# Attention traced without raised scheduling priority in a one-core attention and mLSTM layer

## The chip, the core and the metric

The kernel runs on one core of a Trainium2 chip. The metric is the device time of one execution in microseconds (us). A core has five engines with a queue each: TensorE (PE, the matmuls; its weight loads are shown as PEld), VectorE (DVE), ScalarE (ACT), GpSimd (POOL) and SyncE (SP, which issues most DMAs). Each engine runs its own instructions in the order in which they stand in its queue; between engines semaphores make an instruction wait.

## The reference

One layer of a diffusion backbone: 128 prompt tokens and 1024 latent tokens, width 1024. From one normalised input it projects grouped-query attention (8 query heads of 64, 2 key/value heads) and a bidirectional mLSTM (4 heads of 128, in chunks of 128 tokens), joins both by an output projection, and ends with a SwiGLU FFN of width 2816.

```python
def attention(q, k, v):              # blocks of 128 queries
    def one_block(qi):
        s = jnp.einsum('bqhgd,bkhd->bhgqk', qi, k).astype(F32) * ATTN_SCALE
        p = jax.nn.softmax(s, axis=-1).astype(v.dtype)
        return jnp.einsum('bhgqk,bkhd->bqhgd', p, v)
...
def trunk_layer(...):
    h = rmsnorm(x, norm1_w) * (1 + sc1) + sh1
    aq, ak, av, mq, mk, mv, mo, mg = jnp.split(h @ w_in, SPLIT_POINTS, axis=-1)
    ...
    attn_o = attention(aq, keys, vals)
    ...
    hm, st_f, st_b = mlstm_bidir(heads(mq), heads(mk) * (MLSTM_DK ** -0.5), heads(mv), gates, init_f, init_b)
    ...
    x = x + g1 * (jnp.concatenate([attn_o, hm], axis=-1) @ w_out)
    h2 = rmsnorm(x, norm2_w) * (1 + sc2) + sh2
    x = x + g2 * swiglu(h2, w_gu, w_down)
```

The prompt's queries see the 128 prompt keys; the latent queries see 1024 latent keys and 128 cached ones, 1152 in all.

## The kernel before

**Who sets the order.** The kernel is written as Python generators, each of which emits some instructions and yields. `weave` and `beside` step a main generator and take steps of side generators between its own, at given rates. What is emitted is a trace; a scheduler then simulates the engines and picks for each engine, among the instructions that are ready in its simulation, the one with the best place in the traced order. `hot(n)` (line 59) is `tc.high_priority(n)`: what is traced inside it gets a place n instructions ahead of where it was traced. So the final order of every queue hangs on these numbers. Instructions outside such a block keep their traced place.

**Attention** (`attention`, line 1088) is a side generator. The nine blocks of 128 queries are cut in three chunks of three, `attention(0..2)`, and `chain` puts them one behind the other. The first block is the prompt's. For each of the eight heads of a block:

- six matmuls write the scores S of 128 x 1152 into PSUM (line 1129); there is one buffer for S, so the next head's scores must wait until the exp has read the last one;
- DVE takes the row maximum (1131), ACT the exponential with its row sum into `pr` (1132), DVE two tiny operations for the scale (1133, 1134);
- ACT writes the weights' float16 high part `ph` (1135), DVE the remainder `pl` (1136);
- SP issues a transposing DMA for each, to `phT` (1138) and `plT` (1139).

For each pair of heads a group of 18 matmuls then multiplies the transposed weights with the values (1153 with phT, 1154 with plT, in turn), and ACT and DVE copy the result out (1156, 1158). The generator emits a pair's values one step after the scores of the next pair's second head, so that the transposes have time. In the text the 72 head passes are called S1 to S72 and the 36 values groups V1 to V36, in the order of the program; Vn belongs to S2n-1 and S2n. At the start of a block the queries are transposed by PE (124).

The first parameter after `done`, `ha`, is the priority of the queries, scores, softmax and transposes; the second, `hv`, that of the values group. Before, chunks 0 and 1 have 200 and 0, and chunk 2 has the defaults 200 and 200.

**What runs beside it.** The main work in the order of the program:

- the mLSTM heads: `head_project` (projection products, lines 526 to 528, and 866 to 868) and `head_mlstm` (products 842, 912 to 915, 946, 953), with one attention step for every four or five steps of them;
- the output projection of the first chunk, woven with the last mLSTM scan;
- the prefill of the first FFN chunk, with an attention step at every third of its steps;
- the first FFN pass: gate and up products (1473 to 1475), down products (1215 to 1217), with the splitting of each weight tile into a high part `whi` (ACT, line 174) and a low part `wlo` (DVE, line 145). `attention_side` is woven into it: first the output projection of chunk 1, then what is left of attention.

When attention has ended, its pools are closed, and the second FFN pass begins.

Of the kernel before, what the change touches and what calls it, by code (L numbers as in the profile page):

```python
# [33 lines left out]
CB = 3  # L34
# [15 lines left out]
def hybrid_step(ctx: ExitStack, tc: tile.TileContext, I: dict, O: dict):  # L50
# [15 lines left out]
    def weave(main, side, n_main, n_side):  # L66

        due = 0.0
        for units in main:
            due += n_side / n_main * (units or 1)  # L70
            while due >= 1.0:
                next(side, None)
                due -= 1.0
# [5 lines left out]
    def chain(*gens):  # L79
        for g in gens:  # L80
            for v in g:
                yield v
# [34 lines left out]
    o_d = [drp.tile([P, 512], F32, name=f"o_d{i}") for i in range(2 * CB)]  # L117
# [872 lines left out]
    def beside(*sides):  # L990

        due = [0.0] * len(sides)
        while True:
            for i, (g, rate) in enumerate(sides):
                due[i] += rate
                while due[i] >= 1.0:
                    next(g, None)
                    due[i] -= 1.0
            yield
# [737 lines left out]
    oT = []  # L1737
    done = set()
    o1 = []
    att0 = attention(0, oT, done, 200, 0)  # L1740
    o2 = []
    att = chain(att0, attention(1, o1, set(), 200, 0, o_d[0:CB]), attention(2, o2, set(), spill=o_d[CB:]))
    weave(head_project(0, sts[0]), beside((chain([None] * 10, att), 0.2),), 96, 96)
    for h in range(1, NH):
        scan = head_mlstm(h - 1, sts[h - 1])
# [176 lines left out]
```

## Time and profile before

| | |
|---|---|
| runs, us | 1533.99, 1530.81, 1533.54 |
| median, us | 1533.54 |
| profiled execution, us | 1534.27 |
| its span, us | 1532.5 |
| PE busy | 1429.3 us, 93% of the span, 8282 matmuls |
| DVE, ACT, POOL busy | 74%, 53%, 14% |

A row of the timeline reads: start (us from the span's start), duration, engine, line, operation, what it writes <- what it reads, shapes, how many in a row, and in brackets how long the engine stood idle before it and what released it. SPq is the issue of a DMA on SP's queue. A row of the stretches lists start and end, then for each engine the busy us and the number of its instructions, then PE's granted clock (1.00 is full speed), the share of the DMA engines' time, and GB/s. Starts of matmuls lie closer than their durations, since PE overlaps them.

### The profile page before, as it was taken

What the parts mean: (1) busy time and instruction counts of PE and PEld (TensorE: products, weight loads), DVE (VectorE), ACT (ScalarE), POOL (GpSimd) and SP (SyncE); (2) the same over time, 40 slices, a digit from 0 to 9 for tenths busy, and PEclk for the clock granted to TensorE, in tenths of its full rate; (3) what the DMA queues carried; (4) which work ended last, traced back from release to release, by engine and by line L of the source; (5) the groups of instructions that cost most, each with busy time, mean ns of one, the idle gap of its engine ahead of it and who ended that gap; (6) DMA issues with size and microseconds to landing.
All of it is one profiled execution on the core that took longest, in us unless ns stands there. A gap on an engine that the chain in (4) does not pass through costs nothing. (4 is left out here: it accounts for less than half of the span.)

```text
span 1532.5 us, 22792 instructions
## 1 busy us (share of the span) xinstructions
PE 1429.3 (93%) x8282; PEld 1064.6 (69%) x8282; DVE 1129.3 (74%) x2280; ACT 812.6 (53%) x1525; POOL 213.8 (14%) x310
## 2 busy tenths in 40 slices
PE   6889999998899789999999889999999999999994
PEld 3635667766677567978998777976766667676763
DVE  4968556775767978658677755979878696886857
ACT  4854467956767646555575743844334151523233
POOL 0122423231224345210100000000000000000000
PEclk9999999999999999999999989999999999999998
DMA  9575224653477774758687733444222140412112
GB/s 370 157 217 183 80 70 75 128 110 56 95 152 163 190 213 106 205 177 213 174 195 174 174 92 131 131 142 155 69 80 87 31 134 1 138 49 76 35 35 83
DMA packets 254182, 197.02 MB, mean 129 GB/s; under 512 B 166830, under 2 KB 208006, under 8 KB 254070
## 3 DMA queue, kind: packets, MB, share of 16 engines
q1 hardware_dynamic: 251070, 189.56, 45.7%
q10 hardware_dynamic: 2872, 5.62, 1.1%
q8 instruction: 65, 1.06, 0.3%
q14 instruction: 47, 0.39, 0.1%
q0 software_dynamic: 128, 0.39, 0.1%
HBM read 143.94 MB, written 13.26 MB: 103 GB/s over the span
## 5 line engine op out<-in xcount | busy, mean ns | idle before, releaser
L1621 PE MATMUL mm<-Bt,A 128*128 128x384 f16 x616 | 200.8, 326 | 0.0
L1620 PE MATMUL mm<-Bt,A 128*128 128x384 f16 x616 | 199.5, 326 | 0.8 <-DVE c L1641 0.8
L1622 PE MATMUL mm<-Bt,A 128*128 128x384 f16 x616 | 197.6, 326 | 0.0
L174 ACT CAST whi<-raw 128x1024 fp32r<-128x1024 f32 (+1 forms) x102 | 102.8, 1012 | 138.9 <-DMA raw<-in_w_down_dram 50.7
L145 DVE TENSOR_TENSOR wlo<-raw,whi 128x1024 fp32r<-128x1024 f32 (+1 forms) x102 | 121.4, 1190 | 52.2 <-ACT whi L174 46.5
L1136 DVE SCALAR_TENSOR_TENSOR pl<-pr,st,ph 128x1152 f16<-128x1152 f32 (+1 forms) x72 | 95.7, 1329 | 36.2 <-ACT ph L1135 36.2
L1473 PE MATMUL mm<-aTh,whi 128*128 128x384 f32 x352 | 120.6, 343 | 1.5 <-DVE F L1564 1.1
L1475 PE MATMUL mm<-aTh,wlo 128*128 128x384 f32 x352 | 120.0, 341 | 0.0
L1474 PE MATMUL mm<-aTl,whi 128*128 128x384 f32 x352 | 119.7, 340 | 0.0
L1132 ACT ACTIVATE pr<-S,st 128x1152 f32<-128x1152 f32 (+1 forms) x72 | 81.5, 1132 | 53.9 <-DVE st L1131 52.7
L1131 DVE TENSOR_REDUCE st<-S 128x1 f32<-128x1152 f32 (+1 forms) x72 | 88.8, 1234 | 22.7 <-PE S L1129 22.6
L526 PE MATMUL wi<-headw,hT 128*128 128x384 f16 x288 | 94.6, 328 | 1.2 <-ACT th L816 1.2
L1129 PE MATMUL S<-kst,qT 128*128 128x384 f32 (+1 forms) x400 | 87.6, 353 | 7.8 <-ACT pr L1132 7.8
L527 PE MATMUL wi<-headw,hT 128*128 128x384 f16 x288 | 94.6, 328 | 0.0
L528 PE MATMUL wi<-headw,hT 128*128 128x384 f16 x288 | 94.5, 328 | 0.0
L1135 ACT ACTIVATE ph<-pr,st 128x1152 f16<-128x1152 f32 (+1 forms) x72 | 83.8, 1163 | 17.1 <-DVE st L1134 8.4
L1620 PEld LDWEIGHTS <-A 128*128 128x128 f16 x616 | 60.2, 98 | 42.6 <-issue 3.3
L1621 PEld LDWEIGHTS <-A 128*128 128x128 f16 x616 | 60.3, 98 | 39.9 <-issue 0.9
L1622 PEld LDWEIGHTS <-A 128*128 128x128 f16 x616 | 60.2, 98 | 39.9
L1606 ACT ACTIVATE A<-S,six 128x1024 f16<-128x1024 f32 x44 | 49.9, 1145 | 68.6 <-PE mm L1622 54.8
L1204 DVE TENSOR_TENSOR t<-mm,hmr 128x512 f32<-128x512 f32 x84 | 54.3, 683 | 39.7 <-PE mm L1690 33.3
L1129 PEld LDWEIGHTS S<-kst,qT 128*128 128x128 f32 x400 | 70.4, 192 | 11.7 <-ACT pr L1132 9.5
(460 smaller groups left out, 3691.7 us busy)
## 6 DMA issues: line engine op xcount, KB each, us to landing
raw<-in_w_gu_dram SPq DMA_DIRECT2D x88, 512.0 KB, 3.6
raw<-in_w_down_dram SPq DMA_DIRECT2D x40, 512.0 KB, 3.9
a<-in_w_ada_dram SPq DMA_DIRECT2D x24, 512.0 KB, 5.5
iraw<-in_w_in_dram SPq DMA_DIRECT2D x32, 256.0 KB, 3.4
x<-in_x_sample_dram SPq DMA_DIRECT2D x11, 512.0 KB, 5.9
raw<-in_w_out_dram SPq DMA_DIRECT2D x10, 512.0 KB
aw<-in_w_ada_dram SPq DMA_DIRECT2D x8, 512.0 KB, 5.4
aw<-in_w_ada_dram SPq DMA_DIRECT2D x16, 256.0 KB, 7.9
```

The source lines that it names most:

```text
L145: (dve if eng == "dve" else pool).tensor_tensor(out=out, in0=full, in1=hi, op=ALU.subtract)
L174: nc.scalar.copy(hi[:, :n], raw[:, :n])
L526: mm(ps[:, :n], ah, wh[:, k % 2, c0 : c0 + n], start=(k == 0), stop=False)
L527: mm(ps[:, :n], ah, wl[:, k % 2, c0 : c0 + n], start=False, stop=False)
L1129: mm(S[:, n, 0:w], qT[:, h, :], kst[kv][:, t, c0 + n * w : c0 + (n + 1) * w], start=(t == 0), stop=(t == 1))
L1136: dve.scalar_tensor_tensor(out=plv, in0=prv, scalar=st[:, 3:4], in1=phv, op0=ALU.mult, op1=ALU.subtract)
L1473: mm(ps, wh[:, k, :], th[:, k, :], start=(k == 0), stop=False)
L1474: mm(ps, wh[:, k, :], tl[:, k, :], start=False, stop=False)
L1475: mm(ps, wl[:, k, :], th[:, k, :], start=False, stop=(k == KD - 1))
L1620: mm(ps, wh[:, k], bt[:, 0, k], start=first and k == 0, stop=False, skip_group_check=True)
L1621: mm(ps, wh[:, k], bt[:, 1, k], start=False, stop=False, skip_group_check=True)
L1622: mm(ps, wl[:, k], bt[:, 0, k], start=False, stop=k == 3, skip_group_check=True)
```

## The change

Attention of all three chunks gets `ha` = 0 and `hv` = 0: no instruction of it is traced inside a raised priority. Nothing else is edited.

```diff
-    att0 = attention(0, oT, done, 200, 0)
+    att0 = attention(0, oT, done, 0, 0)
     o2 = []
-    att = chain(att0, attention(1, o1, set(), 200, 0, o_d[0:CB]), attention(2, o2, set(), spill=o_d[CB:]))
+    att = chain(att0, attention(1, o1, set(), 0, 0, o_d[0:CB]), attention(2, o2, set(), 0, 0, o_d[CB:]))
```

So of chunks 0 and 1 the queries, scores, softmax and transposes lose their 200 places, and of chunk 2 the values groups too. The same instructions are issued; the order of rows changes on all five queues from the first attention block to the end of the first FFN pass. Three places follow. A row is the line, the operation, and written <- read; `S` are scores, `kst` keys, `qT` queries, `wi` the result of a projection, `mm` or `po` other results in PSUM; numbers tell tiles apart.

PE in the second mLSTM head's stretch, from S15 (S_584) to S16 (S_604), before:

```order
L1129 MATMUL S_584_3406<-kst1_1040,qT_442_2821 128x384 x6
L527 LDWEIGHTS hT2_452
L527 MATMUL wi_641_3648<-headw2_1845,hT2_452 128x384
...
L528 MATMUL wi_641_3648<-headw3_1846,hT2_452 128x384
L842 MATMUL mm_592_3438<-wv_591_3435,kt_585_3421 128x258
L946 MATMUL mm_596_3448<-cs_343_2417,qT_251_1991 128x129
L946 MATMUL mm_596_3448<-cs_381_2559,qT_251_1991 128x129
L1129 MATMUL S_604_3480<-kst1_1040,qT_442_2821 128x384 x6
```

And now:

```order
L1129 MATMUL S_584_3406<-kst1_1040,qT_442_2821 128x384 x6
L527 LDWEIGHTS hT2_452
L527 MATMUL wi_641_3648<-headw3_1846,hT2_452 128x384
L528 LDWEIGHTS hT2_452
L528 MATMUL wi_641_3648<-headw3_1846,hT2_452 128x384
L842 MATMUL mm_592_3438<-wv_591_3435,kt_585_3421 128x258
L946 MATMUL mm_596_3448<-cs_343_2417,qT_251_1991 128x129
L946 MATMUL mm_596_3448<-cs_381_2559,qT_251_1991 128x129
L1129 MATMUL S_604_3480<-kst1_1040,qT_442_2821 128x384 x6
```

Eight projection products stood between the two scores, and two stand there now: S15 has moved back past six of them, S16 has not moved.

PE at the end of attention, from S71 (S_1966) to V35 (po_1972), before:

```order
L1473 MATMUL mm_2010_10101<-aTh_1453_7241,whi_2013_10104 128x384
L1474 MATMUL mm_2010_10101<-aTl_1454_7242,whi_2013_10104 128x384
L1475 MATMUL mm_2010_10101<-aTh_1453_7241,wlo_2014_10105 128x384
L1129 MATMUL S_1966_9811<-kst1_1040,qT_1881_9437 128x384 x6
L1129 MATMUL S_1971_9830<-kst1_1040,qT_1881_9437 128x384 x6
L1153 LDWEIGHTS vs_1038
L1153 MATMUL po_1972_9845<-phT_1944_9736,vs_1038 128x256
```

And now, a little earlier, around S70 (S_1957), with V34 (po_1958):

```order
L1129 MATMUL S_1950_9742<-kst1_1040,qT_1881_9437 128x384 x6
L1474 MATMUL mm_1994_10004<-aTl_1454_7242,whi_2000_10040 128x384
...
L124 MATMUL mm_2007_10085<-ident_91,t2_2006_10083 128x128 x4
L1153 LDWEIGHTS vs_1038
L1153 MATMUL po_1958_9782<-phT_1915_9608,vs_1038 128x256
L1129 MATMUL S_1957_9767<-kst1_1040,qT_1881_9437 128x384 x6
L1154 LDWEIGHTS vs_1038
L1154 MATMUL po_1958_9782<-plT_1916_9609,vs_1038 128x256
```

Before, the end was S69, 17 gate/up products, V34 (18 products), S70, four transposes, 24 gate/up products, S71, S72, V35, V36. Now it is S69, five gate/up products, the four transposes, the first product of V34, S70, the other 17 of V34, 17 gate/up products, S71, seven gate/up products, V35, S72, V36.

DVE at the same place, as one piece of the difference (- before, + now):

```order
+L1158 SCALAR_TENSOR_TENSOR oS_1941_9700<-po_1972_9845,vsc_100,ol_1973_9864 64x128 x2
+L1131 TENSOR_REDUCE st_1970_9829<-S_1971_9830 128x1
 L1136 SCALAR_TENSOR_TENSOR pl_1964_9809<-pr_1962_9807,st_1965_9810,ph_1963_9808 128x1152
-L1131 TENSOR_REDUCE st_1970_9829<-S_1971_9830 128x1
 L1133 RECIPROCAL st_1970_9829<-st_1970_9829 128x1
 L1134 TENSOR_SCALAR st_1970_9829<-st_1970_9829 128x1
-L1158 SCALAR_TENSOR_TENSOR oS_1941_9700<-po_1972_9845,vsc_100,ol_1973_9864 64x128 x2
 L1136 SCALAR_TENSOR_TENSOR pl_1969_9828<-pr_1967_9826,st_1970_9829,ph_1968_9827 128x1152
```

The maximum of S72 has moved ahead of `pl` of S71, and V35's copy out ahead of both.

## The prediction

> **What bounds the kernel now.** I read the profile page first, then stretches of 25 us for the engines, then what TensorE (PE) waited for, then single instructions on PE, VectorE (DVE), ScalarE (ACT) and the SP queue. The page's busy line and two lines of its slices:
>
> ```profile
> PE 1429.3 (93%) x8282; PEld 1064.6 (69%) x8282; DVE 1129.3 (74%) x2280; ACT 812.6 (53%) x1525; POOL 213.8 (14%) x310
> PE   6889999998899789999999889999999999999994
> PEclk9999999999999999999999989999999999999998
> ```
>
> PE is busy for 93% of the span, so a new order of the same 8282 matmuls can only change where PE stands still. The change can act only from the first attention block to the end of the first FFN pass, about 900 us. The stretches (start:end, length, busy time of PE, weight loads, DVE, ACT, POOL, then granted clock, DMA share, GB/s):
>
> ```profile
> 275.00:300.00 25.00, 22.67 (x148) 16.62 (x146) 19.28 (x37) 23.16 (x61) 6.73 (x16) 1.00 0.75 169
> 425.00:450.00 25.00, 25.00 (x171) 18.51 (x169) 16.70 (x39) 15.70 (x40) 7.29 (x18) 1.00 0.53 103
> 825.00:850.00 25.00, 25.00 (x150) 22.62 (x149) 20.72 (x30) 16.59 (x25) 0.00 (x0) 1.00 0.82 206
> 850.00:875.00 25.00, 19.69 (x115) 18.14 (x114) 17.31 (x26) 20.82 (x30) 2.60 (x2) 0.96 0.77 177
> 875.00:900.00 25.00, 15.22 (x68) 11.58 (x67) 11.91 (x26) 9.84 (x18) 0.00 (x0) 0.70 0.32 71
> ```
>
> Where PE is full (425 to 450 us, and in the FFN pass 825 to 850), attention lies wholly beside other matmuls and a better order has nothing to win. What can be won is at the places where PE ran out of other work: spots in the mLSTM heads such as 275 to 300 us, and 850 to 900 us, the tail of attention, where the last FFN products of the pass have been used up. What PE waited for from 300 to 920 us (total us, times, longest):
>
> ```profile
> PE S L1129 <- ACT pr L1132: 7.0, 5, 3.8
> PE po L1153 <- DMA phT<-ph: 5.6, 2, 5.3
> PE mm L1153 <- DMA phT<-ph: 3.5, 2, 2.2
> PE mm L1153 <- ACT th L816: 2.4, 1, 2.4
> PE po L1154 <- DMA plT<-pl: 2.6, 3, 1.1
> PE mm L1154 <- DMA plT<-pl: 1.2, 2, 1.0
> ```
>
> Attention's own waits are these two kinds: a score group that waits for the exp of the head before it (there is one score buffer), and a values group that waits for the transposed weights. They sum to 22.3 us: more than that the change cannot give, and most of it stands in the tail.
>
> **How long the two chains are.** Number the 72 head passes S1 to S72 and the 36 values groups V1 to V36 (V of pair n belongs to S2n-1 and S2n). One score to the next, at S15 and S16:
>
> ```profile
> 275.14 1.35 PE L1129 MATMUL S<-kst,qT 128*128 128x384 f32 x6
> 276.94 1.36 DVE L1131 TENSOR_REDUCE st<-S 128x1 f32<-128x1152 f32 x1
> 278.69 1.24 ACT L1132 ACTIVATE pr<-S,st 128x1152 f32<-128x1152 f32 x1
> 276.33 0.34 PE L527 MATMUL wi<-headw,hT 128*128 128x384 f16 x1
> 276.50 0.33 PE L528 MATMUL wi<-headw,hT 128*128 128x384 f16 x1
> 280.08 1.32 PE L1129 MATMUL S<-kst,qT 128*128 128x384 f32 x6 [0.76 <-ACT pr L1132]
> ```
>
> S15 ends at 276.49, the max and the exp follow, and S16 starts at 280.08: 3.6 us between two scores are the price of the chain here, with 0.76 of it not covered. The best it could be is the max and the exp alone, 1.36 + 1.24 = 2.6; with DVE busy elsewhere it is longer (6.4 at S67, below). Score to values, at S34:
>
> ```profile
> 434.62 1.35 PE L1129 MATMUL S<-kst,qT 128*128 128x384 f32 x6
> 436.79 1.35 DVE L1131 TENSOR_REDUCE st<-S 128x1 f32<-128x1152 f32 x1
> 438.18 1.22 ACT L1132 ACTIVATE pr<-S,st 128x1152 f32<-128x1152 f32 x1 [0.35 <-DVE st L1131]
> 440.43 1.26 ACT L1135 ACTIVATE ph<-pr,st 128x1152 f16<-128x1152 f32 x1
> 441.73 1.42 DVE L1136 SCALAR_TENSOR_TENSOR pl<-pr,st,ph 128x1152 f16<-128x1152 f32 x1 [0.68 <-ACT ph L1135]
> 443.17 1.31 SPq L1139 DMA_TRANSPOSE plT<-pl  x1
> phT<-ph SPq DMA_TRANSPOSE x26, 3.4
> plT<-pl SPq DMA_TRANSPOSE x25, 3.7
> ```
>
> From 435.97 to 443.17 + 3.7 = 446.9 are 10.9 us. Back to back with no queue the pieces are 1.35 + 1.22 + 1.26 + 1.42 + 3.7 = 9.0.
>
> **The change part by part.** No instruction is added or removed; rows change places on all five queues. I count the PE work that the order puts between the end of one score group and the next, or its values, before and after, with the spacings of the trace: 0.17 us for a projection (276.33 to 276.50), 25.00/150 = 0.17 for a gate/up product, 0.11 for a values product (345.12 to 345.23, below). Where the work is shorter than the chain, PE waits for the rest.
>
> *Removed.* Three waits of the heads:
>
> ```profile
> 345.12 0.27 PE L1154 MATMUL mm<-plT,vs 128*128 128x256 f16 x1 [0.99 <-DMA plT<-pl]
> 345.23 0.27 PE L1153 MATMUL mm<-phT,vs 128*128 128x256 f16 x1
> 359.37 0.28 PE L1153 MATMUL mm<-phT,vs 128*128 128x256 f16 x1 [2.21 <-DMA phT<-ph]
> 400.43 1.32 PE L1129 MATMUL S<-kst,qT 128*128 128x384 f32 x6 [1.60 <-ACT pr L1132]
> ```
>
> S30 (400.43) has 2.1 us of work ahead of it before and 6.2 after: its 1.60 goes. V11 (345.12) gets 9.2 us for 8.7, and V12 (359.37) 6.3 for 5.8: 0.5 each. Sum -2.6. Nothing is late behind S30, because S31 now follows it more closely, which I count next.
>
> *New score waits in the heads,* at 3.6 us per chain. S16 loses six projections of its cover, 6 x 0.17 = 1.0, and it waited already, so all of that is paid: +1.0. S13 goes from 6.0 to 3.1 us of cover: +0.5. S31 from 5.4 to 3.0: +0.6. S39 from 3.8 to 2.4: +1.2. Sum +3.3. If the chain took its bare 2.6 us, S16 would pay about 1.0 and S39 0.2; at S67's length each of the four would pay about 3. What is queued behind each is more PE work of the heads, a product of the mLSTM (L953) first, and so the mLSTM waits with it.
>
> *New values waits in the heads,* at 10.9. V17 goes from 10.9 to 9.7 (+1.2), V18 from 12.1 to 10.4 (+0.5), V19 from 11.9 to 9.4, of which S39's own wait pays 1.2 (+0.3), V6 from 13.7 to 10.8 (+0.1). Sum +2.1. At 9.0 us all four are nothing; at V27 to V32 of the FFN pass, where the distances move by tens of us, nothing comes near a limit.
>
> *First FFN pass up to 850 us.* PE is full, so there is no wait to remove. DVE and ACT are not free, though; at S67:
>
> ```profile
> 834.78 1.22 PE L1129 MATMUL S<-kst,qT 128*128 128x384 f32 x6
> 839.11 1.35 DVE L1131 TENSOR_REDUCE st<-S 128x1 f32<-128x1152 f32 x1
> 841.18 1.20 ACT L1132 ACTIVATE pr<-S,st 128x1152 f32<-128x1152 f32 x1
> ```
>
> From 836.00 to 842.38 the chain takes 6.4 us, because the splits of the weights (L174, L145) stand ahead of it. The order puts 5.1 us before S68 where there were 8.5: +1.3. V33 has 13.6 us for 15.8 in a stage where the score's chain is some 3 us over its bare length, so 10.9 + 3.2 = 14.1: +0.5. Sum +1.8; bounds 0 (a chain of 3.6) and +4.
>
> *The tail.* Its rows before:
>
> ```profile
> 854.41 1.22 PE L1129 MATMUL S<-kst,qT 128*128 128x384 f32 x6
> 872.59 1.96 PE L1129 MATMUL S<-kst,qT 128*128 128x384 f32 x6 [3.79 <-ACT pr L1132]
> 885.08 0.37 PE L1153 MATMUL po<-phT,vs 128*128 128x256 f16 x1 [5.34 <-DMA phT<-ph]
> 886.33 0.39 PE L1154 MATMUL po<-plT,vs 128*128 128x256 f16 x1 [0.88 <-DMA plT<-pl]
> ```
>
> From the end of S69 (855.6) V36 starts 29.5 us later. In the new order I follow the chain from there. Five gate/up products, four transposes and one product of V34 take 1.6 us; S70 waits until 3.6 and ends at 4.8. The rest of V34 (17 x 0.11) and 17 gate/up products end at 9.6; S71 ends at 10.8, seven products at 12.0. V35 needs the weights of S70: 4.8 + 10.9 = 15.7, and ends at 17.7 (18 x 0.11). Only then comes S72, ending at 18.9. Its chain to the landing of ph's transpose took 885.08 - 874.55 = 10.5 us before, where S72's max stood behind pl of S71 on DVE and its ph behind V35's copy on ACT. In the new order the max is ahead of pl of S71, and V35's copy is ahead of everything. The bare chain is 1.35 + 1.22 + 1.26 + 3.4 = 7.2, and with the 1.42 of pl of S71, which still stands ahead of the reciprocal, 8.6; between that and 10.5 I take 9.4. V36 then starts at 28.3, that is 1.2 earlier than 29.5. Two waits are moved, from S72 (3.79) and V36 (5.34) to S70 (2.0), V35 (3.7) and V36 (9.4); the matmuls are the same. If S70's chain is as slow as S67's, 2.8 us over, the tail is 1.6 longer than before; with both chains bare it is 4 shorter. I take -1.
>
> Sum: -2.6 + 3.3 + 2.1 + 1.8 - 1.0 = **+3.6 us**. The profiled execution took 1534.27 us (span 1532.5 and 1.77 around it), so 1537.9; the median of the runs, 1533.54, lies 0.73 below that execution, which gives **1537.1**.
>
> **The clock.** After V12's wait of 2.21 us the next 3.4 us ran at:
>
> ```profile
> 360.40:363.80 3.40, 3.21 (x18) 2.27 (x17) 0.42 (x1) 0.87 (x4) 0.00 (x0) 0.59 0.01 2
> ```
>
> So a wait of 2.2 us costs 0.41 x 3.4 = 1.4 us more here. The Trainium skill, in TensorE: Matmul & The Clock Gate, section "HAM oscillation — how this bites in real kernels", puts the limit at idle gaps of about 3.4 us; by that rule the new waits of the heads would leave the clock alone and the sum would stay. The trace's 0.59 after 2.21 us does not bear this rule out.
>
> **The rivals.** *The chains are shorter than I took them, and the tail is won* (faster). With the scores at 2.6 us and the values at 9.0, the new waits shrink to S16 and S39, +1.2, those of the FFN pass to 0, and the tail gives its 4: -2.6 + 1.2 - 4 = -5.4, 1528. It decides from a score chain below 3 us and a values chain below 9.5. For it: ACT and DVE do the work of the mLSTM earlier, so its waits could shrink too (the wait on th L816, 2.4, is one I left alone). Against: 10.9 and 3.6 were measured in these same stages. Chance 0.25.
>
> *The waits take each other's place.* A wait paid at S13 or S39 gives the following chains the same time, as I reckoned only at V19; removed and new waits of the heads then cancel (-2.6 + 3.3) and so do FFN pass and tail: 1534, within 0.2%. That is also the outcome if the new order is as good as the old and nothing else. For it: the full stretches, and the same total of work. Chance 0.30.
>
> *The new waits take the clock down* (slower still). S16 then waits 0.76 + 1.0 = 1.8 us and its neighbour before it 0.4, S39 and V19 1.5 within 10 us: two places near the 2.21 us of V12, 1.4 us each, and in the tail S70 and V35 wait before the FFN products that ran at 1.0 before S72: 17 + 7 of them at 0.59, 24 x 0.17 x 0.7 = 2.8. Sum 3.6 + 2.8 + 2.8 = +9.2, 1543. It decides from waits of about 2 us. Against: the 0.76 of S16 left 1.00 in its stretch, 275 to 300 us, and a shorter chain undoes it. Chance 0.15.
>
> **How the numbers follow.** The forecast has 0.30: 1537, its own range 1534.5 to 1541. A measurement of this kernel can tell about 0.2%, 3.1 us: 1530.5 to 1536.6 counts as the same. The forecast lies on that border, with a third of its chance in the same band. Faster: 0.25 from the first rival, less a fifth that stays within the band, plus a little from the second: 0.24. Slower: 0.2 + 0.15 + 0.05 from the second: 0.40. Same: 0.36. The range from 1528 to 1544 takes in the price at bare chains and that with the clock.
>
> **What would show it.** S30 without its wait; S16 with about 1.8 us and S39 with 1.2 on the exp; V17 and V18 with about a us on their transposes; S68 with a wait in a stretch that was full; in the tail V36 starting 28 us after the end of S69, with S72 behind V35. It is wrong if the score chain in the new order is far from 3.6 us, because DVE and ACT now serve others first or because they are freer, if the mLSTM's own waits change by more than 2 us, or if the tail moves by more than 2 us.

## The result, and the profile after

The changed kernel takes 1543.28 us (median of 4 runs, 1541.97 to 1543.9), the kernel before 1532.88 in the runs beside them. The ratio is 1.0064, with a 95% interval of 1.0049 to 1.0078: slower by 10 us. The profiled execution has a span of 1541.2 us, 8.7 more than before. The busy line and the clock's slices of its page:

```profile
PE 1430.9 (93%) x8282; PEld 1068.1 (69%) x8282; DVE 1128.3 (73%) x2280; ACT 814.5 (53%) x1525; POOL 218.0 (14%) x310
PEclk9899999999999899999999989999999999999998
```

The same matmuls, and all but the same busy time. To see where the time went I took the start of the n-th matmul of each line in both traces and followed by how much it lags. Where attention's own matmuls changed places most, in the mLSTM heads, it grows by 3 us up to V13 (386 us), and most of that is gone again by 511 us, where the two kernels stand level. It grows by 7 us between 511 and 610 us, where the PE order of the two kernels is alike but for a few rows: the last mLSTM scan, the first output projection and the prefill, from the gate products behind S45 (line 382) to the transposes of the prefill between S48 and S49 (line 124). From here on, "the stretch". S46 to S48 and V22 to V24 lie in it. Its row in the kernel before (start:end, length, then busy us of PE, weight loads, DVE, ACT, POOL, granted clock, DMA share, GB/s):

```profile
511.67:602.84 91.17, 80.32 (x456) 61.18 (x457) 75.43 (x205) 46.76 (x101) 38.95 (x35) 0.97 0.66 181
```

and after:

```profile
511.75:609.89 98.14, 83.62 (x456) 64.18 (x456) 74.45 (x205) 46.09 (x101) 41.48 (x35) 0.91 0.61 169
```

456 matmuls in both. PE stands still for 98.14 - 83.62 = 14.5 us instead of 91.17 - 80.32 = 10.9, and it is busy 3.3 us longer with the same work, because the clock is at 0.91 instead of 0.97. So about half of the 7 us is waiting and half is clock. What PE waited for in this stretch, in the rows that changed, before (total, times, longest):

```profile
PE mm L1251 <- DVE fl L1462: 2.3, 2, 2.1
PE mm L1251 <- ACT mx L1297: 1.8, 1, 1.8
PE wi L946 <- ACT it L949: 1.6, 1, 1.6
...
PE mm L493 <- ACT hmx L484: 0.9, 1, 0.9
PE mm L124 <- ACT t L1452: 0.6, 1, 0.6
...
PE wi L953 <- DVE nu L956: 0.4, 1, 0.4
```

and after:

```profile
PE mm L124 <- ACT t L1452: 3.0, 1, 3.0
...
PE mm L1251 <- ACT mx L1297: 2.9, 1, 2.9
PE wi L946 <- ACT it L949: 2.6, 1, 2.6
PE mm L493 <- ACT hmx L484: 1.5, 1, 1.5
...
PE wi L953 <- DVE nu L956: 1.1, 1, 1.1
...
PE mm L1251 <- DVE fl L1462: 0.4, 1, 0.4
```

None of these waits is attention's. They are the mLSTM scan's (it, nu), the norm's maximum for the gate (hmx), the mixing's (mx) and the prefill's (t, fl): work of ACT and DVE, whose queues have another order here. Of attention's own waits, three rows of PE's timeline in the heads and two in the tail answer to those shown before:

```profile
272.79 0.28 PE L1154 MATMUL mm<-plT,vs 128*128 128x256 f16 x1 [1.17 <-DMA plT<-pl]
282.79 1.31 PE L1129 MATMUL S<-kst,qT 128*128 128x384 f32 x6 [1.46 <-ACT pr L1132]
294.04 0.71 PE L953 MATMUL mm<-va,sd 128*128 128x129 f32 x4 [1.40 <-ACT it L949]
...
863.98 1.22 PE L1129 MATMUL S<-kst,qT 128*128 128x384 f32 x6
...
893.01 0.37 PE L1153 MATMUL po<-phT,vs 128*128 128x256 f16 x1 [8.01 <-DMA phT<-ph]
```

V6 waits 1.17 (272.79), where it did not wait before, S16 waits 1.46 for 0.76 (282.79), and a product of the mLSTM behind them waits 1.40. S30's wait of 1.60 is gone. S69 is the row at 863.98, V36 the one at 893.01.

### The profile page after: what moved, and what is told of

Its sections match the earlier page's. It is cut to its first block, busy times and chain, and to the rows that moved or that the text cites. A ratio compares the mean times of both kernels' runs of the same rounds, so it can differ in the third digit from the quotient of the medians.

```text
span 1541.2 us, 22782 instructions
## 1 busy us (share of the span) xinstructions
PE 1430.9 (93%) x8282; PEld 1068.1 (69%) x8282; DVE 1128.3 (73%) x2280; ACT 814.5 (53%) x1525; POOL 218.0 (14%) x310
## 5 line engine op out<-in xcount | busy, mean ns | idle before, releaser
L1620 PE MATMUL mm<-Bt,A 128*128 128x384 f16 x616 | 199.4, 326 | 0.7 <-DVE c L1641 0.7
L145 DVE TENSOR_TENSOR wlo<-raw,whi 128x1024 fp32r<-128x1024 f32 (+1 forms) x102 | 121.1, 1187 | 44.9 <-ACT whi L174 38.9
L1620 PEld LDWEIGHTS <-A 128*128 128x128 f16 x616 | 60.2, 98 | 42.5 <-issue 3.3
L1688 PE MATMUL mm<-whi,hl 128*128 128x512 f32 x192 | 76.9, 401 | 0.0
```

What stands on the lines that cost most here:

```text
L145: (dve if eng == "dve" else pool).tensor_tensor(out=out, in0=full, in1=hi, op=ALU.subtract)
L1620: mm(ps, wh[:, k], bt[:, 0, k], start=first and k == 0, stop=False, skip_group_check=True)
L1688: mm(ps, hl[:, 0, sl], wh[:, k % 2, :], start=(k == 0), stop=False)
```

## The experiments

Twelve runs, in three sets; in each the kernel before ran beside them on the same chip. The first question was whether the 7 us of the stretch were made by the order there (theory A) or were the chance of one execution (B), against the prediction's own terms (C). Theory A was formed from the lag, so it needed a second profile and kernels that have one part of the change alone.

**The changed kernel again.** No edit.

> The changed kernel once more, for a second profile. Theory A (the loss is made between 500 and 610 us, by the changed order of ACT and DVE there: later waits, and the clock at half for 20.5 us instead of 6.8): the lag to the kernel before again grows by 6 to 9 us between 500 and 610 us, with the same waits (it L949 2.6, mx L1297 2.9, t L1452 3.0), and the time is again 9 to 11 us over before. Theory B (these half-clock stretches were the chance of one execution): waits as in the first profile, but the half clock there is 7 to 14 us, the lag of the stretch 3 to 5, and the missing rest shows elsewhere.

Measured: 1540.91 us against 1530.56, ratio 1.007 (1.0056 to 1.0084). The stretch took 98.06 us (507.58 to 605.64), against 98.14 in the first profile, with the same waits: 2.55 on it L949, 2.97 on mx L1297, 2.96 on t L1452, granted clock 0.91. So it is no chance, and B falls.

**Chunk 0 alone, chunk 1 alone, chunk 2 alone.**

```diff
 c0:
-    att0 = attention(0, oT, done, 200, 0)
+    att0 = attention(0, oT, done, 0, 0)
 c1:
-    ... attention(1, o1, set(), 200, 0, o_d[0:CB]) ...
+    ... attention(1, o1, set(), 0, 0, o_d[0:CB]) ...
 c2:
-    ... attention(2, o2, set(), spill=o_d[CB:]))
+    ... attention(2, o2, set(), 0, 0, o_d[CB:]))
```

> Only attention of chunk 0 (S1 to S24) without priority. Its order of ACT and DVE differs from before also between 500 and 560 us, though none of its attention runs there. Theory A: +3 to +6 us, all of it between 500 and 560 us; the heads from 200 to 360 us alone about 0. Theory B and the terms of the prediction (S13, S16, V6: +1.6, V11 and V12: -1.0): +0.6.

> Only chunk 1 (S25 to S48) without priority. Its order of ACT and DVE differs over the whole of 500 to 610 us. Theory A: +5 to +8 us, made there, with the heads from 360 to 500 us about 0 (S30's wait and a half-clock stretch go, S31, S39 and V17 to V19 come). Terms of the prediction: S30 -1.6, S31 and S39 +1.8, V17 to V19 +2.0: +2.2.

> Only chunk 2 (S49 to S72) without priority; its order differs only from about 700 us on. Theory A: +1 us (FFN pass -0.7, tail +1.7, as in the profile after). Prediction: +1.8 for the FFN pass, -1 for the tail, +0.8. Theory B, if the heads and 500 to 610 us cost little: up to +8, in the tail.

Measured: chunk 0 alone 1.0067 (1.0053 to 1.008), +10 us; chunk 1 alone 1.0038 (1.0025 to 1.0051), +6; chunk 2 alone 0.9996 (0.9984 to 1.0008), nothing. The parts sum to 16 us and the whole is 10, so chunk 0 and chunk 1 seem to share a loss that is paid once; each ratio is uncertain by some 2 us, which leaves its size open. The stretch is such a loss: 96.44 us with chunk 0 alone and 96.46 with chunk 1 alone, 92.82 with chunk 2 alone. The order says why it is shared: ACT's and DVE's rows of the scan come out the same, word for word, in both, and unlike those of before, though chunk 0's attention is long over by then. The prediction's terms for chunk 0 (+0.6) and chunk 1 (+2.2) are far off. For chunk 0 there is more than the stretch; that is taken up in the next section.

**Two head passes alone, and two others.** Two kernels each take the priority from two of the 72 head passes only:

```diff
 s29_30:
-                with hot(ha):
+                with hot(0 if b == 3 and 4 <= h < 6 else ha):
 s31_32:
-                with hot(ha):
+                with hot(0 if b == 3 and 6 <= h < 8 else ha):
```

> Only two of the 72 head passes, S29 and S30, lose their priority; S30's wait in the heads goes, and the orders of ACT and DVE in the last mLSTM scan (500 to 560 us) come out as in the changed kernel. Theory A (the scan's order carries the loss): from the first gate product after S48 (line 382) to the last prefill transposes that wait on t (line 124) 96 to 97 us, as with chunk 0 or 1 alone, against 91 to 93 before, half clock there 13 to 14 us; the time +4 to +6 us. Theory C (attention's own waits in the heads carry it): S30's wait of 1.6 us is gone, so 0 to -3 us.

> Only S31 and S32 lose their priority: the heads' order changes in 28 places on PE, but the last scan keeps the order of before on ACT, DVE and PE. Theory A: within 0.15% of before, the stretch 91 to 93 us. Theory C, by S31's 0.6 us and S32: +1. A rival D, that any change of the order costs some us: +4.

Measured: S29 and S30 alone 1.0034 (1.0022 to 1.0046), +5 us; S31 and S32 alone 1.0 (0.9988 to 1.0012). The stretch of the first:

```profile
507.96:604.14 96.18, 82.68 (x456) 62.41 (x456) 73.84 (x205) 47.26 (x103) 40.76 (x35) 0.93 0.62 172
```

and of the second:

```profile
506.51:599.24 92.73, 81.50 (x457) 61.83 (x457) 74.43 (x205) 46.99 (x101) 39.91 (x35) 0.94 0.64 178
```

Two head passes, which end 100 us before the stretch begins and whose own wait (S30) went away, cost 5 us; two others, next to them, cost nothing, though they move rows in 28 places. The difference between the two is whether the scan's order changes. Theory C said 0 to -3 for the first and +1 for the second. Rival D, that any other order costs, falls with the second.

**Block 5 alone, and the queries of block 1 alone.**

```diff
 blk5:
-                with hot(ha):
+                with hot(0 if b == 5 else ha):
 q_blk1 (the transposes and copies of the queries, not the heads):
-            with hot(ha):
+            with hot(0 if b == 1 else ha):
```

> Only the eight heads of block 5 (S41 to S48) lose their priority. Heads and last scan keep the order of before; only the first output projection and prefill (550 to 610 us) get the changed kernel's order on ACT and DVE. Theory A: the later half of the loss alone: t L1452 waits 3.0 instead of 0.6, fl L1462 0.4 instead of 2.1, the stretch 92 to 94 us, the time +1 to +2 us. Rival: the prefill is the whole of it, +5.

> Only the query transposes and copies of block 1 lose their priority. The heads' order changes in 75 places on PE, and the last scan gets a third order, unlike both kernels' (ACT differs from before in 6 places, DVE in 16, where the changed kernel has 9 and 30). Theory A says the time follows the scan's waits: if the wait on it L949 is 2.5 as in the changed kernel, +3 to +6 us, if 1.7 as before, 0 to +1, whatever the heads did. Rival D: +4 in any case.

Measured: block 5 alone 0.9996 (0.9985 to 1.0008), with the stretch at 93.41 us and t L1452 at 2.97: the wait of the prefill came as expected, fl L1462 fell from 2.1 to under 0.3, and the time did not move. So the changed order of output projection and prefill alone costs about a us in the stretch, below what the times can tell; the rival that it is the whole is out. Block 1's queries alone came out faster, 0.9969 (0.9954 to 0.9984), -5 us, with a third order in the scan. There the wait on it L949 is gone, and in its place PE waits 1.15 and 0.73 on nu L956; the stretch took 91.79 us. I had expected 0 to +1 at best.

**One reason for the longer waits in the scan: a multiply on GpSimd.** The timelines of DVE and POOL in the scan, in the kernel before:

```profile
522.36 2.11 DVE L136 TENSOR_SCALAR rh<-rv 128x3 int32<-128x3 int32 x1
...
522.32 2.11 POOL L977 TENSOR_TENSOR hm<-hm,ry 128x1152 f32<-128x1152 f32 x1 [0.31 <-DVE rv L135]
```

and after:

```profile
524.22 0.16 DVE L136 TENSOR_SCALAR rh<-rv 128x3 int32<-128x3 int32 x1
524.34 2.04 DVE L963 TENSOR_TENSOR dn<-dn,QT 128x2 f32<-128x2 f32 x1
...
524.24 2.11 POOL L977 TENSOR_TENSOR hm<-hm,ry 128x1152 f32<-128x1152 f32 x1
...
528.39 0.71 PE L946 MATMUL wi<-cs,qT 128*128 128x129 f32 x4 [2.56 <-ACT it L949]
```

Line 136 takes 0.16 us in the second fence, and 0.16 is also the median of line 963 in this trace (36 times, on 128x2 elements). Here they take 2.11 and 2.04, about the length of the multiply on POOL that began 0.04 or 0.1 us before and ended with them. The Trainium skill, in SBUF — State Buffer, section "SBUF: two separate sides", describes a pair of ports that VectorE and GpSimd share under an exclusive lock, which the one that starts first holds for its whole instruction; on VectorE's side it is taken by operations with two SBUF inputs, or in a mode that uses two ports. The rows of dn, which has two SBUF inputs, agree with it; line 136 has one, and whether it ran in such a mode no run here shows. Before, the held operation stood in the norm of the scan's first three blocks; after, it begins 2 us later and stands in the denominator dn, from which the next chain hangs: dn, hm on ACT (L966) and DVE, its square on ACT (L969), and behind that the copy it (L949), for which PE waits 2.56 instead of 1.65. To test it I cut the multiply into nine of one block each, in three kernels; the fourth run repeats the fast kernel. The loop is written shorter here than in the kernel.

```diff
 s29_split (on s29_30), a_split (on the changed kernel), b_split (on the kernel before):
-                    pool.tensor_tensor(out=v, in0=v, in1=bc(r, 2, [P, n, P]), op=ALU.mult)
+                    for p0 in range(0, n, w): pool.tensor_tensor(out=v[:, p0 : p0 + w], in0=v[:, p0 : p0 + w],
+                        in1=bc(r[:, p0 : p0 + w], 2, [P, w, P]), op=ALU.mult)   # w is 1 in the third head, else n
 q_split: q_blk1 again
```

> S29 and S30 without priority, as in the run before, and GpSimd's multiply of the third head's nine blocks (line 977, 2.11 us) cut into nine of one block; nothing left out. The orders of ACT and DVE in the last scan stay word for word those of S29 and S30 alone. Theory A1 (this multiply holds off the tiny DVE operation beside it, line 963, for 2.04 us, in the chain that PE waits for on it L949): no DVE operation of line 963 over 0.6 us, the wait on it L949 1.0 to 1.6 instead of 2.55, half clock in the stretch 7 to 10 us instead of 13.7, the stretch 92 to 94 instead of 96.2, the time +0.5 to +3 us over before instead of +5. Theory A2 (the place of the operations in the queues costs the time, not the stall): wait and time as without the cut, +5.

> The changed kernel with the same cut of line 977 into nine. A1: 2 to 4 us less than the changed kernel, +6 to +8 over before, the stretch 94 to 96 instead of 98.1; the rest, heads and tail, stays. A2: +10.

> The kernel before with the same cut. There the multiply held off line 136 (2.11 us) in another chain, with a wait of 1.65 on it L949. A1: that wait down to about 1, the time 0 to -2 us. A2: 0.

> The kernel with only block 1's query transposes and copies without priority, a second time and with no other edit (no cut), since it came out faster than before by 0.31%. If that is its order: again -3 to -6 us. If it was the chance of that set of runs: within 1 us of before.

Measured: with the cut, S29 and S30 alone cost 1.0009 (0.9992 to 1.0027), +1.4 us instead of +5. Its DVE, POOL and PE rows in the scan, and the stretch:

```profile
520.93 0.32 DVE L963 TENSOR_TENSOR dn<-dn,QT 128x2 f32<-128x2 f32 x1
...
520.85 3.30 POOL L977 TENSOR_TENSOR hm<-hm,ry 128x128 f32<-128x128 f32 x9
...
523.83 0.71 PE L946 MATMUL wi<-cs,qT 128*128 128x129 f32 x4 [1.39 <-ACT it L949]
...
509.46:604.05 94.59, 81.68 (x456) 61.48 (x456) 72.61 (x205) 47.37 (x103) 41.89 (x43) 0.95 0.65 175
```

The held operation takes 0.32 us, the wait on it is 1.39, nu's fell from 1.09 to 0.43, and the clock is 0.95 for 0.93, with ACT's and DVE's rows of the scan unchanged. The stretch is 1.6 us shorter, less than the 2 to 4 expected: hmx L484 waits 2.0 instead of 1.5, which fits nine multiplies that take 3.3 us for 2.1, and a wait of 1.8 of the transposes (L124) on nu, which the kernel before does not have, stays. So the hold is shown as the cause of the longer waits on it and nu. What it costs in time is not: the times fell by 3.6 us, but the intervals of the two ratios (1.0022 to 1.0046 and 0.9992 to 1.0027) overlap, and 1.6 us is no more than the stretch differs between executions of one order (91.17 and 92.82 with the order of before).

In the changed kernel the cut gave 1.0059 (1.0036 to 1.0082), 8 to 9 us over before, not to be told from the 10 without it. Its profiled execution was the longest of its nine (span 1552.0). Even so the wait on it fell there to 1.39 and that on nu to 0.43, while hmx rose from 1.5 to 2.8, and the stretch was no shorter:

```profile
516.55:616.64 100.09, 85.64 (x456) 64.25 (x456) 73.30 (x205) 46.84 (x103) 41.93 (x43) 0.90 0.59 165
```

In the kernel before the cut gave 0.9992 (0.9978 to 1.0006), nothing. Its wait on it fell to 1.25, but its stretch took 94.85 us, with a wait of 1.6 on sd L920 that was not there and 1.6 for 0.5 on mx L145: the cut changed the order behind it.

The queries of block 1 alone gave 0.9975 (0.9961 to 0.9989) the second time, after 0.9969. This version beats the kernel before by 4 to 5 us. Where from is open: its stretch took 91.79 and 92.02 us, no better than the 91.17 of the kernel before's one profile, and what it wins is spread over heads and tail by less than its profiles scatter.

## Why the prediction was right or wrong

The direction and the range held (1528 to 1544 against 1543.28), the forecast of 1537 was a third of the way: +3.6 us were reckoned and 10 came. The table sets the profiles side by side. First column: how much longer than before it takes from the start of S1 to the start of V13. Then the us from V13 to the stretch, the stretch, and from it to the first product of line 1620 in the second pass.

| kernel | ratio | heads to V13 | V13 to stretch | stretch | to L1620 |
|---|---|---|---|---|---|
| before | 1 | 0 | 125.9 | 91.2 | 424.6 |
| s31_32 (scan as before) | 1.0000 | -0.6 | 123.0 | 92.7 | 427.8 |
| blk5 (scan as before) | 0.9996 | -0.1 | 124.1 | 93.4 | 423.2 |
| c2 (scan as before) | 0.9996 | -0.3 | 123.2 | 92.8 | 424.7 |
| s29_30 | 1.0034 | -0.2 | 124.8 | 96.2 | 425.2 |
| c1 | 1.0038 | -0.5 | 124.7 | 96.5 | 422.3 |
| c0 | 1.0067 | +3.1 | 125.8 | 96.4 | 423.0 |
| changed | 1.0064 | +3.0 | 123.5 | 98.1 | 426.2 |
| changed, again | 1.0070 | +1.5 | 123.4 | 98.1 | 425.8 |

The heads and the stretch together give 7 of chunk 0's 10 us; for the rest its one profile shows no place.

*What bounds it.* Right: PE is full in the FFN pass in both, and all that moved is standing still and clock. Two rows after:

```profile
275.00:300.00 25.00, 20.13 (x130) 14.47 (x129) 19.19 (x39) 22.95 (x55) 5.39 (x12) 1.00 0.66 149
825.00:850.00 25.00, 25.00 (x132) 21.91 (x131) 22.27 (x34) 16.62 (x25) 0.03 (x1) 1.00 0.78 198
```

Wrong in one sentence: that attention's own waits are what the change can touch. It can touch every wait in the 900 us, because the scheduler places all instructions anew after a change. (The 22.3 us there also take in V13's 2.4, which the row puts down to the mLSTM's th.)

*The step that failed* is the count itself, "I count the PE work that the order puts between the end of one score group and the next, or its values". It saw only attention's rows on PE. The stretch, where PE's order hardly moves, did not come into the sum at all; there ACT's and DVE's orders moved, and it cost 98.1 less the mean 92.2 of before, s31_32 and c2: 5.9 us, most of what came. Of this the scan's order makes 4 (c0, c1 and s29_30 lie at 96.2 to 96.5). The rest, 1.7, is not made by the order of the stretch: but for rows at its edge, chunk 1 alone has there the same order as the changed kernel on PE, ACT, DVE and POOL, and yet takes 96.46 us:

```profile
506.90:603.36 96.46, 82.42 (x456) 62.70 (x457) 74.65 (x205) 46.67 (x103) 40.76 (x35) 0.93 0.59 172
```

The traces differ in the clock: half speed for 13.7 us there, and for 17.1 in both profiles of the changed kernel. Why that is so stays open. The last paragraph of the prediction named the mLSTM's own waits as what would make it wrong, without a price.

*Removed.* S30's wait went, as reckoned. V12's is 2.10 and 2.08 in the two profiles, for 2.21, where half a us less was reckoned; V11's is 0.49 and 0.97, for 0.99.

*New score and values waits in the heads*: of the eight, two came. S16 waits 1.46, reckoned 1.8 from the six projections it lost. V6, reckoned at 0.1, waits 1.17. S13, S31, S39, V17, V18 and V19 have no wait above 0.35 us in the trace. One length for all chains was the error. The exps ahead of S16, S31 and S39 end 2.65 us after the score before them, as the first rival had it, and those ahead of S31 and S39 took 2.7 in the trace before already, where those ahead of S13 and S16 took 3.4 and 3.5. V17 to V19 start 9.2 to 10.0 us after their second score without a wait, while V6's second product waits until 12.8. What stood behind S16 waited too, on it L949 (1.40), and so the heads to V13 cost 1.5 to 3.0, all from chunk 0 (c0: 3.1), which the sum had put at +0.6. After V13 nothing is lost. The 125.9 of before goes with its clock, 0.86 from 375 to 400 us:

```profile
375.00:400.00 25.00, 20.61 (x117) 15.10 (x116) 18.33 (x41) 20.73 (x44) 5.45 (x13) 0.86 0.46 74
```

Chunk 0 alone, in the same order there, also has 0.86 and takes 125.8; chunk 2 and block 5 alone, again in that order, have 1.00 and take 123.2 and 124.1, and the changed kernel has 1.00 and takes 123.5 and 123.4. So one order gives times 2 to 3 us apart here from one execution to the next.

*Luck.* The heads were reckoned at +2.8 in all (-2.6 + 3.3 + 2.1), near the 1.5 to 3.0 that came, but chunk 1's share of that came to nothing, as far as these rows tell, and chunk 0 made it all. And the range held a loss made in a place that no term or price stood for.

*FFN pass and tail.* Reckoned +1.8 and -1.0, and chunk 2 alone came out at -0.6 us (-2.4 to +1.2). The last column scatters from 422.3 to 427.8, so single terms can't be read from it. S68 has no wait, where 1.3 us was reckoned. The tail's length came out near: from the end of S69 to V36 it takes 893.01 - 865.20 = 27.8 us, reckoned 28.3, before 29.5. Its parts did not: S70 does not wait (reckoned 2.0), V35 waits 1.9 in all (3.7) and V36 8.0 (9.4). And S69 itself starts 9.6 us later than before, more than the 6.1 that the FFN's products lag at 825 us: twelve more of the FFN's products stand ahead of it, which leaves fewer beside the chain, and that was left out.

*The rivals.* The first, "the chains are shorter", had the score chains right (2.65 us at three of the four places), and the time rose all the same. 1543 was the price of "the new waits take the clock down". The number was hit, not the reason: the clock in 275 to 300 us, around S16, is 1.00 in the trace after, as before, and in the tail both traces have 17 us at half speed. It fell in the stretch, to 0.91: from 529.9 to 536.7 us, for one, the row of the stretches has 0.50, and in all some 17 of the 98 us ran at half speed. The longest wait there is 3.0 us. The Trainium skill, in TensorE: Matmul & The Clock Gate, section "HAM oscillation — how this bites in real kernels", gives as its rule that there be no idle gaps above about 3.4 us; the prediction set that against the 0.59 after a wait of 2.21, and this stretch bears the trace out, with every wait below that limit.

## What to carry to other kernels

A scheduler's priority is not a local edit: it reorders engines far behind the code that carries it, so compare the orders of all engines over the whole program, and price the stretches where ACT or DVE moved, even where TensorE's order did not. Look there for what each engine's small operations now stand beside; a 2 us operation on GpSimd may hold a 0.16 us operation on VectorE, and whether that costs anything depends on which chain it hits. And since neighbouring orders differed here by 5 us both ways, in one case for a reason that stayed open, and since profiles of one order differ by 2 to 3 us in one place, with the clock, a change of order is judged by repeated times of several such orders, not by one.

## What was not expected of the hardware

Removing the priority of two head passes (S29, S30) cost 5 us, and removing it from the transposes and copies of one block's queries gained 4 to 5, twice measured. A one-input VectorE operation on 128x3 integers was held for 2.11 us by a multiply on GpSimd, as a two-input one on 128x2 was for 2.04. And half of the stretch's loss is not waiting but clock: 456 matmuls were busy for 80.32 us at 0.97 and for 83.62 at 0.91.
